# Projection stage of a hybrid decoder step: half 0 as three 256-column matmuls per weight tile, and the sample's convolution taps and pooling sums on GpSimd

## The chip, the cores and the metric

The kernel runs on one core of one Trainium2 chip. The metric is the device time of one execution in microseconds (us), the median of several runs. A profiled execution gives a trace: one record for each instruction on each engine. The engines are PE (TensorE, with PEld for its weight loads), DVE (VectorE), ACT (ScalarE), POOL (GpSimd) and SP (SyncE, which here issues the DMAs). Each engine takes its instructions in the order in which they stand in its own queue.

## The reference

One layer of a decoder step in float32, for 1024 prompt tokens and 8 x 8 sample tokens:

```
x = x + 0.5 * swiglu(rmsnorm(x, norm_ffn1), ffn1_w_in, ffn1_w_out)
hn = rmsnorm(x, norm_mix)
proj = hn @ w_in                       # 1024 -> 8224: u, z, xbc, dt, gate logits
u_ext = [pool_hist, u]                 # trailing-window means of 2, 4, 8, 16 rows, minus u
xp = [conv_hist, xbc]                  # y = b + sum_k xp[:, k:k+T] * w[k];  silu(y)
...                                    # pooling branch, SSD scan, gates, out projection
x = x + mix
x = x + 0.5 * swiglu(rmsnorm(x, norm_ffn2), ffn2_w_in, ffn2_w_out)
y = rmsnorm(x, norm_final)
```

The outputs are y, the last 15 rows of `u_ext`, the last 3 rows of `xp` (the new pooling and convolution states) and the SSD states. The change touches the product `hn @ w_in` and what is done with u and xbc right after it.

## The kernel before

Channels lie on the partitions and tokens along the free dimension. The tokens are worked on as two halves: half 0 holds 512 prompt tokens, half 1 the other 512 and the 64 sample tokens (`NTOK = (512, 576)`).

**Stages.** A first feed-forward block, the projection stage (`in_proj`), the mixing stage (pooling branch, SSD scan, merge, output projection), a second feed-forward block. The projection stage runs in this trace from about 871 us to 1523 us.

**A pair.** `proj_pair` makes two 128-channel rows, `ia` and `ib`, of the projection for both halves by a Winograd-form product: seven products instead of eight, in the order 1, 2, 6, 5, 7, 3, 4 (`PRODUCTS`). There are 29 pairs that hold both halves, and one of half 1 alone: gates (kind g), and in each of four groups three pairs of xbc (kind c), one of u (kind u) and two of z (kind z). So 12 pairs feed the convolution and 4 the pooling.

**A product.** `wino` (line 467) does product p for half 0 and then for half 1, over four 128-row weight tiles k. Float32 accuracy comes from splitting weight and data into a high and a low part, `wh`, `wl` and `xh`, `xl`, and adding wh*xh, wh*xl and wl*xh. Half 1 has 288 columns in a product and does these as three 288-column matmuls, into one range of a PSUM bank. Half 0 has 256 columns. Its high and low parts lie side by side, so that wh*[xh|xl] is one matmul of 512 columns and wl*xh one of 256, and the bank holds two sums of 256 columns that have still to be added. Every matmul loads its own weights. The banks A, B, C of each half are the six buffers of the tag `pd`; A collects products 1, 6, 7 and 4, B product 2, C products 5 and 3.

**Taking the sums out of PSUM.** After each product, `after` calls `leave` (line 1097). For half 1 this is one ACT copy (products 1, 6, 5, 4) or one DVE add (2, 7, 3) of 288 columns into the rows' tiles `ra`, `rb`. For half 0 the copies and adds have 512 columns and go to two scratch tiles `t` and `v` (lines 1120, 1122, 1125, 1127, 1129, 1132), and after products 2, 7 and 3 a POOL add of the two 256-column pieces writes `ra` or `rb` (lines 1123, 1130, 1133). Product 4 of half 0 is an ACT copy and a DVE add of 256 columns (lines 1135, 1136).

**Weights.** `wino_weights` (line 426) makes seven weight tiles of the four raw ones (`wraw`, 6 buffers): four sums `s` on POOL (line 437, 4 buffers), and for each tile a rounded copy `wh` on ACT (line 443) and the rest `wl` on DVE (line 444), 3 buffers each.

**After a row is done** (`done`, after products 3 and 4), work is queued with `post` and fed by a worker between products. `post_conv` does the convolution: ACT makes `b + w0*x` (line 936), DVE adds three taps (line 940), ACT applies silu (line 942) and a DMA writes the result. In half 1 the 64 sample tokens are separate small instructions: POOL copies them with their history into a tile `crs` (lines 931, 932), ACT and DVE do 64-column taps. `post_u` does the window sums by doubling on DVE (line 955; line 959 for the sample, whose rows lie in `urs`), the mean minus u (lines 966, 972) and a split into high and low parts. `state_out` makes the new states: a PE transpose `pst` (line 167) of the last columns of the row's tile, an ACT copy `so` (line 1039), DMAs. In `done` it is queued ahead of `post_conv` or `post_u`.

**Order of the queues.** The program is recorded with a model of time (`tick`, `post`), and a scheduler sets each engine's queue; instructions in `tc.high_priority` blocks (the weights' and `leave`) are drawn ahead. What stands in a queue is fixed before the run.

Of the kernel before, what the change touches and what calls it, by code (L numbers as in the profile page):

```python
# [14 lines left out]
P = 128  # L15
# [46 lines left out]
def tile_hybrid_pool_ssd_macaron(  # L62
# [401 lines left out]
            out.append(raw)  # L464
        return out

    def wino(weights, nk, xs, after):


        banks = [[None] * 3 for _ in xs]  # L470
        for (p, b), (wh, wl) in zip(PRODUCTS, weights):
            for i, (h, X) in enumerate(xs):
                n = NPAIR[h]
                new = banks[i][b] is None
                if new:
                    banks[i][b] = psum("pd", "pw" + p)
                out = banks[i][b][:, :n]
                if h == 0:
                    both = banks[i][b].rearrange("p (a b) -> p a b", a=2)
                    for k in range(nk):  # L480
                        x = X[p][k]
                        mm(both, wh[:, k, :], x, start=new and k == 0, stop=False, free=True)
                        mm(out, wl[:, k, :], x[:, 0, :], start=False, stop=k == nk - 1, free=True)
                    after(p, i, banks[i])
                    tick()
                    continue
                for k in range(nk):
                    xh, xl = X[p][k]
                    for j, (W, x) in enumerate(((wh, xh), (wh, xl), (wl, xh))):
                        mm(out, W[:, k, :], x, start=new and k == 0 and j == 0, stop=k == nk - 1 and j == 2, free=True)  # L490
                after(p, i, banks[i])
                tick()
# [417 lines left out]
    def post(gen):  # L910
        work.append((pe[0] + RIPE, gen))
# [12 lines left out]
    def post_conv(h, ct, raw, new):  # L924
# [11 lines left out]
            S.activation(o, f(0), AF.Identity, bias=cols[:, i_cb + ct : i_cb + ct + 1], scale=w[0])  # L936
        yield POST
        for j in range(1, 4):
            for o, f in parts:
                V.scalar_tensor_tensor(o, f(j), w[j], o, op0=ALU.mult, op1=ALU.add)  # L940
            yield POST
        S.activation(t[:, :N], t[:, :N], AF.Silu)
        dma(convd[h][ct], t[:, :N])
# [2 lines left out]
    def post_u(h, k, raw, smp):  # L946
# [6 lines left out]
        while sh < w:  # L953
# [2 lines left out]
                            cur[:, sh - 1 : HIST + 512 - sh], op=ALU.add)  # L956
            if h == 1:
                nxs = smp[1 + q]
                V.tensor_tensor(nxs[:, :, 2 * sh - 1 :], curs[:, :, 2 * sh - 1 :],
                                curs[:, :, sh - 1 : HIST + NT - sh], op=ALU.add)  # L960
                curs, q = nxs, 1 - q
            yield POST
# [33 lines left out]
    def done(kind, i, h, raw):  # L996
# [25 lines left out]
    outs = {}  # L1022

# [31 lines left out]
    def proj_pair(kind, ia, ib, xs):  # L1055
# [22 lines left out]
        def after(p, i, bk):  # L1078
# [17 lines left out]

        def leave(p, h, n, o, af, as_, bf, bs, *bk):

            f, s_ = slice(0, n), slice(n, 2 * n)
            A, B, C = bk  # L1100
            if h == 1:
                A, B, C = (x[:, :n] if x is not None else None for x in bk)
                if p == "1":
                    S.copy(af, A)
                elif p == "2":
                    V.tensor_tensor(af, B, af, op=ALU.add)
                elif p == "6":
                    S.copy(as_, A)
                elif p == "5":
                    S.copy(bs, C)  # L1110
                elif p == "7":
                    V.tensor_tensor(bs, A, bs, op=ALU.add)
                elif p == "3":
                    V.tensor_tensor(as_, C, as_, op=ALU.add)
                else:
                    S.copy(bf, A)
            else:
                t, v = o["t"][:, : 2 * n], o["v"][:, : 2 * n]
                if p == "1":
                    S.copy(t, A)  # L1120
                elif p == "2":
                    V.tensor_tensor(t, B, t, op=ALU.add)
                    G.tensor_tensor(af, t[:, f], t[:, s_], op=ALU.add)
                elif p == "6":
                    S.copy(v, A)
                elif p == "5":
                    S.copy(t, C)
                elif p == "7":
                    V.tensor_tensor(t, A, t, op=ALU.add)  # L1129
                    G.tensor_tensor(bs, t[:, f], t[:, s_], op=ALU.add)  # L1130
                elif p == "3":
                    V.tensor_tensor(v, C, v, op=ALU.add)
                    G.tensor_tensor(as_, v[:, f], v[:, s_], op=ALU.add)
                else:
                    S.copy(t[:, s_], A[:, s_])
                    V.tensor_tensor(bf, A[:, f], t[:, s_], op=ALU.add)

        wino(wino_weights(W, 0, 4, 4, c0 + ia * P, c0 + ib * P), 4, xs, after)

    def in_proj(prep):  # L1140

# [636 lines left out]
```

## Time and profile before

| | |
|---|---|
| median of 3 runs | 2937.12 us (2936.72 to 2939.24) |
| profiled execution | 2939.05 us, of which the trace's span is 2937.3 us |
| PE busy | 2828.8 us, 96% of the span, 18494 matmuls and as many weight loads |
| DVE busy | 1784.7 us, 61% |
| ACT busy | 1385.2 us, 47% |
| POOL busy | 993.0 us, 34% |
| mean share of 16 DMA engines | 54% |

How to read it: matmuls are pipelined, so each record is longer than the distance to the next one's start; the distance between starts is what a matmul costs in a stream. Shares over the span mix stages with different limits, so the views are asked for the projection stage alone. In the view of groups a line shows the line of the kernel, the engine, the operation, output<-inputs, the shape, the count, then the busy time in us with the mean of one in ns, and the idle time of the engine just before, with what ended it. In the view of waits a line shows who waited for whom: us in total, times, longest us. A timeline's row shows start, duration, engine, line, operation, and the count of merged instructions.

### The profile page before, as it was taken

Reading aid. Unit: us, or ns where it says so; the run is one execution under the profiler, and the core shown is the slowest. Engines: PE = TensorE matmul, PEld = TensorE weight load, DVE = VectorE, ACT = ScalarE, POOL = GpSimd, SP = SyncE. Lnnn points to the kernel's source line nnn. Section 1 sums busy time; section 2 is a strip of 40 time slices with the busy share of each in tenths; the row PEclk is TensorE's granted clock in tenths of the full one; section 3 lists DMA queues with packets and bytes.
Section 4 is the critical chain, followed back from the end, with each engine's and each line's share of the span. In section 5 each row is a group of like instructions: output and inputs, shape, how many; then the busy total and the mean of one; then the engine's idle time right before and its main releaser. Section 6 shows DMA issues by size and latency. Waiting matters only on the chain.

```text
span 2937.3 us, 51029 instructions
## 1 busy us (share of the span) xinstructions
PE 2828.8 (96%) x18494; PEld 2570.2 (88%) x18494; DVE 1784.7 (61%) x2843; ACT 1385.2 (47%) x3024; POOL 993.0 (34%) x1011
## 2 busy tenths in 40 slices
PE   7999999999999999999989999898999999999998
PEld 6999999789989989898977887677999999987898
DVE  6655555434484687887976877766665544453422
ACT  5444444323354555564556766566233444442422
POOL 6434444000133455454422332323234444440000
PEclk9999999999999999999999999999999999999999
DMA  4575554856445555543367777786774532236652
GB/s 134 166 224 182 160 172 132 277 188 194 112 126 163 159 179 159 183 127 124 98 221 240 235 235 232 229 271 184 237 241 153 161 98 77 81 101 212 218 156 72
DMA packets 530332, 507.97 MB, mean 173 GB/s; under 512 B 36884, under 2 KB 374664, under 8 KB 530072
## 3 DMA queue, kind: packets, MB, share of 16 engines
q1 hardware_dynamic: 530064, 504.72, 54.0%
q8 instruction: 145, 2.38, 0.3%
q14 instruction: 107, 0.88, 0.1%
q10 hardware_dynamic: 16, 0.00, 0.0%
HBM read 361.77 MB, written 143.05 MB: 172 GB/s over the span
## 4 chain that ended last, share of the span: by engine, by line
PE 44%; DVE 6%; ACT 3%; DMA 3%; issue 1%; POOL 1%; SPq 1%; POOLq 0%; ACTq 0%; DVEq 0%
PE pw L163 19%; PE po L163 9%; PE pso L163 4%; PE pwo L163 3%; PE pbp L163 3%; PE pg L163 1%; PE pu L163 1%; ACT ab L1357 1%; PE pyd L163 1%; DVE wl L444 1%; DVE ct L940 1%; PE pst L163 1%; DMA wraw<-in_ffn_w_in_dram 0%; DVE xs L1504 0%; DVE ab L1359 0%
## 5 line engine op out<-in xcount | busy, mean ns | idle before, releaser
L163 PE MATMUL pw<-X,wh 128*128 128x288 f32 (+1 forms) x2484 | 624.0, 330 | 11.9 <-ACT t L1120 5.3
L163 PE MATMUL pw<-X,wl 128*128 128x288 f32 (+1 forms) x1644 | 472.9, 288 | 0.8 <-DVE wl L444 0.8
L163 PEld LDWEIGHTS pw<-X,wh 128*128 128x128 f32 x2484 | 417.7, 188 | 51.5 <-ACT t L1120 6.7
L163 PE MATMUL pw<-hl,wh 128*128 128x512 f32 x1072 | 390.5, 398 | 3.1 <-DVE t L1129 2.1
L444 DVE TENSOR_TENSOR wl<-s,wh 128x512 fp32r<-128x512 f32 x288 | 223.3, 776 | 200.6 <-ACT wh L443 179.1
L163 PE MATMUL pw<-hi,wh 128*128 128x288 f32 x1120 | 332.1, 297 | 1.3 <-ACT t L596 1.3
L163 PE MATMUL pw<-lo,wh 128*128 128x288 f32 x1120 | 329.7, 294 | 0.0
L163 PE MATMUL pw<-hi,wl 128*128 128x288 f32 x1120 | 329.6, 294 | 0.0
L295 DVE TENSOR_TENSOR wl<-wraw,wh 128x512 fp32r<-128x512 f32 x228 | 164.2, 721 | 249.2 <-ACT wh L294 236.9
L163 PEld LDWEIGHTS pw<-X,wl 128*128 128x128 f32 x1644 | 310.6, 189 | 1.9 <-DVE wl L444 1.8
L437 POOL TENSOR_TENSOR s<-wraw,wraw 128x512 f32<-128x512 f32 x144 | 196.0, 1361 | 333.7 <-DVE wl L444 216.7
L163 PE MATMUL pw<-hl,wl 128*128 128x256 f32 x1072 | 299.6, 280 | 0.2 <-DVE wl L444 0.2
L294 ACT ACTIVATE wh<-wraw 128x512 fp32r<-128x512 f32 x228 | 137.8, 606 | 326.0 <-PE po L163 229.1
L444 DVE TENSOR_TENSOR wl<-wraw,wh 128x512 fp32r<-128x512 f32 x216 | 177.0, 819 | 123.0 <-ACT wh L443 116.3
L443 ACT ACTIVATE wh<-s 128x512 fp32r<-128x512 f32 x288 | 180.8, 629 | 146.4 <-PE pw L163 139.1
L163 PEld LDWEIGHTS pw<-hl,wh 128*128 128x128 f32 x1072 | 201.9, 188 | 40.6 <-DVE t L1129 2.9
L163 PEld LDWEIGHTS pw<-hi,wh 128*128 128x128 f32 x1120 | 210.1, 188 | 12.6 <-ACT t L596 1.8
L163 PE MATMUL po<-hh,wh 128*128 128x288 f32 (+1 forms) x800 | 211.0, 324 | 3.6 <-ACT hh L355 3.4
L163 PE MATMUL po<-hh,wl 128*128 128x288 f32 (+1 forms) x800 | 210.9, 322 | 0.5 <-DMA wl<-part 0.5
L163 PE MATMUL po<-hr,wh 128*128 128x288 f32 (+1 forms) x800 | 210.9, 323 | 0.0
L163 PEld LDWEIGHTS pw<-lo,wh 128*128 128x128 f32 x1120 | 210.2, 188 | 0.0
L163 PEld LDWEIGHTS pw<-hi,wl 128*128 128x128 f32 x1120 | 210.1, 188 | 0.0
(384 smaller groups left out, 6340.7 us busy)
## 6 DMA issues: line engine op xcount, KB each, us to landing
wraw<-in_ffn_w_in_dram SPq DMA_DIRECT2D x188, 256.0 KB
wh<-part SPq DMA_DIRECT2D x156, 256.0 KB
wl<-part SPq DMA_DIRECT2D x156, 256.0 KB
wraw<-in_w_in_dram SPq DMA_DIRECT2D x144, 256.0 KB
wraw<-in_ffn_w_out_dram SPq DMA_DIRECT2D x120, 256.0 KB
part<-ph SPq DMA_DIRECT2D x80, 256.0 KB
part<-pr SPq DMA_DIRECT2D x80, 256.0 KB
ab<-acsd SPq DMA_DIRECT2D x64, 256.0 KB
```

What stands on the lines that cost most here:

```text
L163: T.matmul(out, lhsT, rhs, start=start, stop=stop, skip_group_check=free)
L294: S.activation(wh, raw, AF.Copy)
L295: V.tensor_tensor(wl, raw, wh.bitcast(F32), op=ALU.subtract)
L437: G.tensor_tensor(t, a, b, op=op)
L443: S.activation(wh, a, AF.Copy)
L444: V.tensor_tensor(wl, a, wh.bitcast(F32), op=ALU.subtract)
L940: V.scalar_tensor_tensor(o, f(j), w[j], o, op0=ALU.mult, op1=ALU.add)
L1357: S.activation(ab[:L, i, :], ab[:L, i, :], AF.Relu, bias=acs[:L, hc + q * hq + i : hc + q * hq + i + 1], scale=-1.0)
```

## The change

Three things change, all in the projection stage.

1. **Half 0's products.** `proj_pair` passes `beside=False` to `wino`. Half 0 then takes the path of half 1: wh*xh, wh*xl and wl*xh are three matmuls of 256 columns into one 256-column range. `leave` loses its branch for half 0: copies and adds of 256 columns go straight into `ra` and `rb`. The tiles `t` and `v`, the 512-column copies and adds and the three POOL adds of each pair are gone. The feed-forward blocks call `wino` as before.
2. **The sample's small work on POOL.** In `post_conv` each 64-column tap of the sample becomes a POOL product into a new small tile `cm` (2 buffers) and a POOL add. In `post_u` the sample's window sums go from DVE to POOL.
3. **`state_out` behind the post.** In `done`, `state_out` is queued after `post_conv` or `post_u`, no longer ahead of it.

```diff
-    def wino(weights, nk, xs, after):
+    def wino(weights, nk, xs, after, beside=True):
...
-                if h == 0:
+                if h == 0 and beside:
                     both = banks[i][b].rearrange("p (a b) -> p a b", a=2)
                     for k in range(nk):
                         x = X[p][k]
                         mm(both, wh[:, k, :], x, start=new and k == 0, stop=False, free=True)
                         mm(out, wl[:, k, :], x[:, 0, :], start=False, stop=k == nk - 1, free=True)
...
                 for k in range(nk):
-                    xh, xl = X[p][k]
+                    xh, xl = X[p][k] if h else (X[p][k][:, 0, :], X[p][k][:, 1, :])
                     for j, (W, x) in enumerate(((wh, xh), (wh, xl), (wl, xh))):
                         mm(out, W[:, k, :], x, start=new and k == 0 and j == 0, stop=k == nk - 1 and j == 2, free=True)
...
         for j in range(1, 4):
-            for o, f in parts:
-                V.scalar_tensor_tensor(o, f(j), w[j], o, op0=ALU.mult, op1=ALU.add)
+            V.scalar_tensor_tensor(t[:, :512], raw[:, j : j + 512], w[j], t[:, :512], op0=ALU.mult, op1=ALU.add)
+            for o, f in parts[1:]:
+                m = small((P, NB, NT), "cm", 2)
+                G.tensor_tensor(m, f(j), w[j].unsqueeze(2).broadcast_to([P, NB, NT]), op=ALU.mult)
+                G.tensor_tensor(o, o, m, op=ALU.add)
             yield POST
...
-                V.tensor_tensor(nxs[:, :, 2 * sh - 1 :], curs[:, :, 2 * sh - 1 :],
+                G.tensor_tensor(nxs[:, :, 2 * sh - 1 :], curs[:, :, 2 * sh - 1 :],
                                 curs[:, :, sh - 1 : HIST + NT - sh], op=ALU.add)
...
             if h == 1:
                 smp = new
+            post(post_conv(h, i, raw, smp))
+            if h == 1:
                 state_out(kind, i, raw[:, 512:579])
-            post(post_conv(h, i, raw, smp))
...
+            post(post_u(h, i, raw, smp))
+            if h == 1:
                 state_out(kind, i, raw[:, 512:591])
-            post(post_u(h, i, raw, smp))
...
-                if h == 0:
-                    out[i].update(t=fx(name="t"), v=fx(name="v"))
...
         def leave(p, h, n, o, af, as_, bf, bs, *bk):
 
-            f, s_ = slice(0, n), slice(n, 2 * n)
-            A, B, C = bk
-            if h == 1:
-                A, B, C = (x[:, :n] if x is not None else None for x in bk)
...
+            A, B, C = (x[:, :n] if x is not None else None for x in bk)
+            if p == "1":
+                S.copy(af, A)
+            elif p == "2":
+                V.tensor_tensor(af, B, af, op=ALU.add)
+            elif p == "6":
+                S.copy(as_, A)
+            elif p == "5":
+                S.copy(bs, C)
+            elif p == "7":
+                V.tensor_tensor(bs, A, bs, op=ALU.add)
+            elif p == "3":
+                V.tensor_tensor(as_, C, as_, op=ALU.add)
             else:
-                t, v = o["t"][:, : 2 * n], o["v"][:, : 2 * n]
-                if p == "1":
-                    S.copy(t, A)
-                elif p == "2":
-                    V.tensor_tensor(t, B, t, op=ALU.add)
-                    G.tensor_tensor(af, t[:, f], t[:, s_], op=ALU.add)
...
+                S.copy(bf, A)
 
-        wino(wino_weights(W, 0, 4, 4, c0 + ia * P, c0 + ib * P), 4, xs, after)
+        wino(wino_weights(W, 0, 4, 4, c0 + ia * P, c0 + ib * P), 4, xs, after, beside=False)
```

The queues show it at three places. On PE, the first state transpose of the stage (`pst`, of row `ra` of the first xbc pair, half 1; `pw` is a product's bank, its number tells the bank). Before, it stands behind half 1's last matmuls of that pair's product 4 (`pw_2031`) and ahead of product 1 of the next pair (`pw_2070`):

```order
L163 MATMUL pw_2031_10998<-hi_9091,wh_11177 128x288
L163 MATMUL pw_2031_10998<-lo_9092,wh_11177 128x288
L163 MATMUL pw_2031_10998<-hi_9091,wl_11178 128x288
L167 MATMUL pst_2063_11215<-ident,ra_11011 67x128
L163 MATMUL pw_2070_11230<-hl_7838,wh_11226 128x512
L163 MATMUL pw_2070_11230<-hl_7838,wl_11227 128x256
L163 MATMUL pw_2070_11230<-hl_7868,wh_11226 128x512
```

Now it stands inside the next pair, behind product 6 of half 0 (`pw_2058` is that pair's bank A of half 0, `pw_2062` that of half 1):

```order
L163 MATMUL pw_2058_11364<-X_8951,wh_11453 128x256 x2
L163 MATMUL pw_2058_11364<-X_8951,wl_11454 128x256
L163 MATMUL pw_2058_11364<-X_8999,wh_11453 128x256 x2
L163 MATMUL pw_2058_11364<-X_8999,wl_11454 128x256
L167 MATMUL pst_2081_11471<-ident,ra_11123 67x128
L163 MATMUL pw_2062_11384<-X_9310,wh_11453 128x288 x2
L163 MATMUL pw_2062_11384<-X_9310,wl_11454 128x288
```

Between the two places lie five half-products (1 and 2 of both halves, 6 of half 0), and each pair of a 512- and a 256-column matmul has become three of 256 columns.

On POOL, one xbc pair's weight sums `s` and what stands between them, before (`ra`, `rb` with `t`, `v` are half 0's adds; `crs` are the copies of the sample):

```order
L437 TENSOR_TENSOR s_2195_11904<-wraw_11823,wraw_11825 128x512
L1123 TENSOR_TENSOR ra_11544<-t_11546 128x256
L437 TENSOR_TENSOR s_2196_11906<-s_2195_11904,wraw_11819 128x512
L931 COPY crs_11846<-hs_9780 128x8x3
L437 TENSOR_TENSOR s_2213_11983<-wraw_11819,wraw_11823 128x512
L437 TENSOR_TENSOR s_2217_12017<-wraw_11821,s_2196_11906 128x512
L1004 MEMSET rb_11545 128x3
L1130 TENSOR_TENSOR rb_11545<-t_11546 128x256
L1005 COPY chist<-rb_11545 128x3
L1007 COPY rb_11569<-chist 128x3
L1133 TENSOR_TENSOR ra_11544<-v_11547 128x256
```

and now, around the four sums of a pair (`cm`, `ct` are the sample's taps):

```order
L942 TENSOR_TENSOR cm_11632<-crs_11589,cols 128x64
L437 TENSOR_TENSOR s_2135_11788<-wraw_11695,wraw_11697 128x512
L437 TENSOR_TENSOR s_2136_11790<-s_2135_11788,wraw_11691 128x512
L437 TENSOR_TENSOR s_2147_11864<-wraw_11691,wraw_11695 128x512
L1007 MEMSET rb_11378 128x3
L437 TENSOR_TENSOR s_2150_11899<-wraw_11693,s_2136_11790 128x512
L943 TENSOR_TENSOR ct_11588<-ct_11588,cm_11609 128x64
L1008 COPY chist<-rb_11378 128x3
L943 TENSOR_TENSOR ct_11588<-ct_11588,cm_11632 128x64
L1010 COPY rb_11398<-chist 128x3
L942 TENSOR_TENSOR cm_11652<-crs_11589,cols 128x64
L943 TENSOR_TENSOR ct_11588<-ct_11588,cm_11652 128x64
```

The 256-column adds are gone from between the sums; six small taps of each sample row have come in, and those of the second row stand behind all four sums of the next pair.

On ACT, the silu of that second row (`ct_11588`) and what follows it now:

```order
L936 ACTIVATE ct_11588<-crs_11589,cols 128x64
L443 ACTIVATE wh_11699<-wraw_11691 128x512
L936 ACTIVATE ct_11678<-ra_11377,cols 128x512
L945 ACTIVATE ct_11588<-ct_11588 128x576
L443 ACTIVATE wh_11743<-wraw_11693 128x512
L936 ACTIVATE ct_11685<-ra_11397,cols 128x512
L1116 COPY rb_11378<-pw_2058_11364 128x256
```

The silu (line 945) waits for the last POOL tap of the fence above, where before it waited for DVE, and the copy that empties half 0's bank A after product 4 (line 1116) stands behind it.

More of the change, by code (lines that the diff above doesn't have):

```diff
@@ L1097, in leave @@
         def leave(p, h, n, o, af, as_, bf, bs, *bk):
-            f, s_ = slice(0, n), slice(n, 2 * n)
-            A, B, C = bk
-            if h == 1:
-                A, B, C = (x[:, :n] if x is not None else None for x in bk)
-                if p == "1":
-                    S.copy(af, A)
-                elif p == "2":
[L1106 to L1116, printed above, removed]
-            else:
-                t, v = o["t"][:, : 2 * n], o["v"][:, : 2 * n]
[L1119 to L1136, printed above, removed]
```

## The prediction

> **What bounds the kernel now.** On the page PE is busy for 96% of the span, so a change pays only by what PE streams or by what it waits for. I asked first for the busy time in stretches of the projection stage:
>
> ```profile
> core 0: us, PE busy (x) PEld busy (x) DVE busy (x) ACT busy (x) POOL busy (x), PEclk, DMA share, GB/s
> 1160.00:1330.00 170.00, 165.18 (x1095) 153.43 (x1094) 148.11 (x225) 95.48 (x196) 87.10 (x109) 1.00 0.47 150
> sum 663.00, PE 646.30 PEld 600.97 DVE 512.71 ACT 356.22 POOL 304.25; mean PE 129.26 PEld 120.19 DVE 102.54 ACT 71.24 POOL 60.85
> ```
>
> In 663 us around the stage PE is idle for 663.0 - 646.3 = 16.7 us. DVE is the next busiest, 77% over all and 148.11/170 = 87% in the second stretch; POOL has 46%. Then the waits of PE in the stage (who waited for whom: us, times, longest):
>
> ```profile
> PE pst L167 <- DVE ra L1114: 6.7, 8, 1.4
> PE pw L163 <- ACT t L1120: 5.3, 5, 3.0
> PE pw L163 <- DVE t L1129: 2.1, 2, 1.3
> PE pw L163 <- DVE wl L444: 1.0, 3, 0.5
> PE pw L163 <- ACT v L1125: 0.4, 1, 0.4
> ```
>
> Together 15.5 us in 19 stops. Eight are the state transpose, which waits for the last DVE add of its row; the others wait for half 0's tiles to leave PSUM or for a low weight part. The timeline shows what the longest stop costs beside its idle time:
>
> ```profile
> 1470.01 0.29 PE L163 MATMUL pw<-hi,wl 128*128 128x288 f32 x1
> 1473.28 0.79 PE L163 MATMUL pw<-X,wh 128*128 128x512 f32 x1 [2.98 <-ACT t L1120]
> ...
> 1474.08 0.63 PE L163 MATMUL pw<-X,wh 128*128 128x512 f32 x1
> ...
> 1474.72 0.63 PE L163 MATMUL pw<-X,wh 128*128 128x512 f32 x1
> ```
>
> A pair of a 512- and a 256-column matmul takes 0.64 us here, against 0.35 us in the stream below: four such pairs at a low rate, 4 x 0.29 = 1.2 us. And each stop loses the overlap of two records, some 0.16 us (a 288-column record is 0.29 us long and the next usually starts after 0.13). What kept ACT was DVE:
>
> ```profile
> 1471.96 0.63 ACT L355 ACTIVATE dh<-dd 128x512 fp32r<-128x512 f32 x1 [4.06 <-DVE dd L970]
> 1472.50 0.24 ACT L1039 COPY so<-pst 79x128 f32<-79x128 f32 x1
> 1472.64 0.58 ACT L1120 COPY t<-pw 128x512 f32<-128x512 f32 x1
> ```
>
> ACT stood 4.06 us for a DVE chain of the pooling, and the copy that PE needed stood behind it. So the stage is PE's stream plus some 20 us of stops (15.5 + 19 x 0.16 + 1.2 = 19.7), and DVE's queue is what is late at most of them.
>
> **The change, part by part.** *PE's stream.* 29 pairs x 7 products x 4 tiles = 812 times a 512- and a 256-column matmul become three of 256. The columns are the same, 768, but there is a third matmul with a third weight load. The trace has no run of 256-column matmuls; its nearest rows are these starts:
>
> ```profile
> 1483.75 0.39 PE L163 MATMUL pw<-hl,wh 128*128 128x512 f32 x1
> 1483.98 0.28 PE L163 MATMUL pw<-hl,wl 128*128 128x256 f32 x1
> ...
> 1485.16 0.29 PE L163 MATMUL pw<-hi,wh 128*128 128x288 f32 x1
> ...
> 1486.76 0.39 PE L163 MATMUL pw<-hl,wh 128*128 128x512 f32 x1
> ```
>
> Four pairs of half 0 take 1485.16 - 1483.75 = 1.41 us, 0.3525 each or 0.459 ns a column; twelve matmuls of half 1 take 1.60 us, 0.1333 each or 0.463 ns a column. Three times 256 at 0.463 is 0.3556 us, 3.1 ns more; 812 times that is +2.5 us, which I take, since 288 columns is the nearest row that repeats one width. The low bound is 0 (0.459 a column). The high bound is three full 288-column distances, 0.400 us, if it is the weight load that sets 0.133 and not the columns: +0.0475 x 812 = +39 us. Against that end speaks
>
> ```profile
> 1644.00 1.05 PE L163 MATMUL pyo<-bc,hst 128*128 128x128 f32 x8
> L163 PE MATMUL pyo<-bc,hst x224: 270/275/421, 1571.1 to 2029.8; 128*128 128x128 f32 x112
> L163 PE MATMUL pw<-hl,wl 128*128 128x256 f32 x1072 | 299.6, 280 | 0.2 <-DVE wl L444 0.2
> ```
>
> Eight matmuls, each with a weight load of the same size, within 1.05 us, with the last record 0.275 long: (1.05 - 0.275)/7 = 0.111 us each, less than the 0.119 that I give one of 256 columns. The Trainium skill's page "TensorE: Matmul & The Clock Gate" (Back-to-back issue gap) speaks against the change too: a warm matmul costs its columns plus a fixed 2.5 ns. By it the third matmul would cost 812 x 2.5 ns = +2.0 us where columns alone say 0; the row of 288 agrees with a small fixed cost.
>
> *State transposes.* They now stand five half-products later, 2 x 1.6 + 3 x 1.41 = 7.4 us by the starts above. Their longest wait was 1.4 us, so all eight should go: 6.7 + 8 x 0.16 = -8.0 us (at worst half, if DVE is late elsewhere: -4.0).
>
> *Work on DVE, ACT and POOL.* The groups in the stage:
>
> ```profile
> L1122 DVE TENSOR_TENSOR t<-pw,t 128x512 f32<-128x512 f32 x29 | 19.8, 682 | 0.9 <-PE pw L163 0.7 <-DMA gd<-rb 0.2
> L1136 DVE TENSOR_TENSOR rb<-pw,t 128x256 f32<-128x256 f32 x29 | 12.1, 418 | 2.3 <-ACT t L1135 1.3
> L940 DVE SCALAR_TENSOR_TENSOR ct<-crs,cols,ct 128x64 f32<-128x64 f32 x72 | 32.2, 447 | 0.0
> L940 DVE SCALAR_TENSOR_TENSOR ct<-crs,cols,ct x72: 267/274/1323, 1006.4 to 1464.7; 128x64 f32<-128x64 f32 x72
> L959 DVE TENSOR_TENSOR urs<-urs x20: 210/326/1385, 1070.8 to 1485.4; 128x176 f32<-128x176 f32 x8, 128x160 f32<-128x160 f32 x6, 128x128 f32<-128x128 f32 x4, 128x64 f32<-128x64 f32 x2
> L1120 ACT COPY t<-pw 128x512 f32<-128x512 f32 x29 | 16.7, 576 | 0.7 <-PE pw L163 0.7
> L1135 ACT COPY t<-pw 128x256 f32<-128x256 f32 x29 | 10.3, 356 | 3.0 <-PE pw L163 2.7
> L1123 POOL TENSOR_TENSOR ra<-t 128x256 f32<-128x256 f32 x29 | 30.4, 1049 | 31.6 <-DVE t L1122 25.0 <-issue 6.6
> L1130 POOL TENSOR_TENSOR rb<-t 128x256 f32<-128x256 f32 x29 | 27.9, 962 | 49.3 <-DVE t L1129 49.3
> L1133 POOL TENSOR_TENSOR ra<-v 128x256 f32<-128x256 f32 x29 | 25.8, 889 | 27.4 <-DVE v L1132 27.3
> L932 POOL COPY crs<-ra 128x64 f32<-128x64 f32 x12 | 3.4, 280 | 1.2
> L437 POOL TENSOR_TENSOR s<-wraw,wraw 128x512 f32<-128x512 f32 x58 | 82.1, 1416 | 142.5 <-DVE wl L444 87.1 <-DMA wraw<-in_w_in_dram 22.2 <-DVE ct L940 13.7
> ```
>
> DVE: three 512-column adds at 0.682 become 256-column ones at the 0.418 of line 1136, whose own add goes: 29 x (3 x 0.264 + 0.418) = 35 us. With the 72 taps (32.2) and the 20 sums (at the median 0.326: 6.5) it loses 74 of its 513 us and falls to 66%. ACT loses 29 x 3 x (0.576 - 0.356) = 19 us. POOL loses 30.4 + 27.9 + 25.8 = 84 us and gains 144 taps and 20 sums. A tap has 64 columns: a copy of that size takes 0.28, and a straight line through the two-input operations of 512 and 256 columns (1.416 and 0.967, the mean of the three) gives 0.63; I take 0.5, so 72 us, and 0.8 for a sum, which the same line gives for 170 columns: 16 us. POOL stays where it was, at 84 gone and 88 come (bounds 56 and 107).
>
> *The other 11 stops* cost 15.5 - 6.7 = 8.8 us, 11 x 0.16 = 1.8 and the slow 1.2, so 11.8 us. They come where DVE, or ACT behind it, is behind; a DVE freed of a seventh of its work, and half-0 copies that wait for no POOL add, should take half of them, -5.9 (bounds 0 and -11.8). ACT's waits on POOL's adds go with these:
>
> ```profile
> ACT ct L936 <- POOL ra L1133: 27.2, 10, 3.8
> POOL s L437 <- DVE wl L444: 94.1, 36, 7.2
> ```
>
> Sum: 2.5 - 8.0 - 5.9 = -11.4, from the profiled 2939.05 to 2927.6. The runs' median is 1.9 lower than that execution, so I forecast **2926 us**. By the bounds without the 39: from 0 - 8.0 - 11.8 = -20 to 2.5 - 4.0 - 0 = -1.5, so 2917 to 2936 on the median. What follows the stage (DMA landings of the mixing stage's first loads) keeps its order, and I give it nothing.
>
> **The rivals.**
>
> *A wait on POOL takes the place of the old ones (slower).* The sample's second row has its taps behind the next pair's four weight sums. These wait for their buffers, last row above: 2.6 us on average, 7.2 at most. The silu on ACT then waits for POOL, and behind it stands the copy that empties bank A of half 0. That bank is needed by the next pair's product 1, half a product (1.6 us) after product 4 ends; from there PE stands. Twelve xbc pairs, each held 3.6 us (2.6 and two taps), lose 12 x 2.0 = 24 us, against which the 8.0 are still won and nothing else: 2937 + 2.5 + 24 - 8 = 2955. For it: the queue order, and that POOL is slow for its size. Against: the sums' buffers come free with products 6 to 3, ahead of product 4. The Trainium skill's "GPSIMD Engine Reference" (Engine selection) is on its side: elementwise work belongs on VectorE, two-input operations are about twice as slow on GpSimd. The trace agrees (0.97 us here against 0.418 for 256 columns).
>
> *The stops only move.* If DVE's lateness is contention with POOL and DMA waits rather than its own load, PE meets the same stops elsewhere: 2937 + 2.5 - 4 = 2936. For it: POOL stays as busy, and the small tap on DVE takes 447 ns on average where its median is 274 and its longest 1323, so DVE is held up now and then by something outside it.
>
> *All stops go*: 2937 - 19.7 = 2917.
>
> *The weight load sets the pace*: +39 - 14 = 2962.
>
> **How the numbers follow.** Forecast 0.44, stops move 0.20, POOL wait 0.22, all gone 0.10, weight load 0.04. A difference under 0.2%, 5.9 us, is about what a measurement of this kernel can't tell from none, so faster means below 2931.2. The forecast's own range (2917 to 2936) is to nine tenths below that: 0.40; with "all gone" 0.50, and 0.03 of the moved stops. Slower, above 2943: the POOL wait, the load, and 0.01 of the moved: 0.27. The rest, 0.20, is the same. Range: 2914 to 2952; it reaches to the POOL case with two thirds of its price.
>
> **What would show it.** In the changed profile: no wait of `pst` for the DVE add of product 3; half-0 matmuls starting 0.117 to 0.119 us apart; DVE near 440 us in the same stretch, POOL near 305; PE's waits in the stage about 6 us. Wrong if the 256-column starts are 0.13 apart (load), if ACT's silu waits on POOL for over 1.6 us again and again with PE waiting for line 1116's copy, or if PE still waits for half 0's copies as long as before.

## The result, and the profile after

| | median of the runs, us | ratio to before, 95% interval |
|---|---|---|
| before (4 runs beside the change) | 2938.18 (2936.72 to 2939.93) | |
| after (4 runs) | 2922.75 (2920.70 to 2923.54) | 0.9945 (0.9932 to 0.9957) |

The change makes the kernel 15.4 us faster. The forecast was 2926, its own range 2917 to 2936. The profiled execution of the changed kernel took 2922.54 us, its span 2920.7. The busy time in the 663 us that the prediction looked at:

```profile
core 0: us, PE busy (x) PEld busy (x) DVE busy (x) ACT busy (x) POOL busy (x), PEclk, DMA share, GB/s
860.00:1523.00 663.00, 654.51 (x5143) 648.93 (x5141) 443.77 (x701) 355.36 (x742) 312.77 (x435) 1.00 0.50 161
```

DVE came down from 513 to 444 us (forecast near 440), POOL went from 304 to 313 (forecast near 305), and the same stretch now holds 17 us of the next stage. ACT, forecast to lose 19 us, stands at 355 after 356; some 10 of the 355 lie in those 17 us. PE's waits from 870 to 1520 us (who waited for whom: us, times, longest):

```profile
PE pxT L167 <- DMA xs<-cv: 3.9, 4, 3.0
PE pgm L163 <- ACT rb L1116: 0.9, 1, 0.9
PE pw L163 <- DVE wl L444: 0.7, 1, 0.7
```

The first two rows belong to the mixing stage's first work. Of before's 15.5 us in 19 stops one stop of 0.7 us is left. Neither the state transposes (`pst`) nor the half-0 copies appear. The first matmul of the mixing stage (`pgm`) starts at 1505.7 us in place of 1523.0.

The stream itself became longer. Eight 256-column matmuls of half 0, on the timeline:

```profile
1049.29 0.28 PE L163 MATMUL pw<-X,wh 128*128 128x256 f32 x1
1049.41 0.28 PE L163 MATMUL pw<-X,wl 128*128 128x256 f32 x1
1049.53 0.40 PE L163 MATMUL pw<-X,wh 128*128 128x256 f32 x2
1049.77 0.28 PE L163 MATMUL pw<-X,wl 128*128 128x256 f32 x1
1049.89 0.40 PE L163 MATMUL pw<-X,wh 128*128 128x256 f32 x2
1050.13 0.28 PE L163 MATMUL pw<-X,wl 128*128 128x256 f32 x1
1050.25 0.27 PE L167 MATMUL pst<-ident,ra 128*67 128x128 f32 x1
```

They take 1050.25 - 1049.29 = 0.96 us, 0.120 each, so three take 0.360 us where the old pair took 0.3525.

The groups of POOL and DVE that answer to those of before:

```profile
L942 POOL TENSOR_TENSOR cm<-crs,cols 128x64 f32<-128x64 f32 x72 | 46.6, 659 | 0.8
L943 POOL TENSOR_TENSOR ct<-ct,cm 128x64 f32<-128x64 f32 x72 | 40.7, 566 | 23.3 <-ACT ct L936 20.5 <-POOL ra L1007 0.7
L1112 DVE TENSOR_TENSOR rb<-pw,rb 128x256 f32<-128x256 f32 x29 | 12.1, 419 | 1.7 <-PE pw L163 1.6
```

A tap's operation on POOL takes 0.57 to 0.66 us on average for 64 columns (0.5 was put in), the shortest 0.29; why they differ so much is seen with DVE's taps below. The feared wait of ACT's silu (line 945) for POOL is there:

```profile
ACT ct L945 <- POOL ct L943: 27.1, 14, 3.2
POOL s L437 <- DVE wl L444: 147.8, 50, 11.9
```

and 11 of its 14 times are longer than the 1.6 us that the prediction named as a sign of being wrong. The other half of that sign, PE waiting for line 1116's copy, is missing in the stage: no stop of PE there follows from it.

To compare kernels I added up, over every PE start from 870 to 1500 us, the distance to the next start beyond 0.233, 0.117 or 0.133 us (after a projection matmul of 512, 256 or 288 columns). What exceeds by over 0.06 us is a stop with its slow matmuls, the rest is the stream. Before: stream -0.5, stops 27.8 us. After: stream +4.8, stops 6.1. The floor of this count is about 5.6, which it gives for a kernel below with no stop of the stage in its list of waits. So some 22 us of stops went, about the 19.7 that the prediction had counted, and 5 to 6 us of stream came. (The floor is 59 distances too long by some 0.1 us each, nearly all of them beside a transpose in the stream.)

### The profile page after: what moved, and what is told of

It is laid out like the page before. It is cut to its first block, busy times and chain, and to the rows that moved or that the text cites. A ratio compares the mean times of both kernels' runs of the same rounds, so it can differ in the third digit from the quotient of the medians.

```text
span 2920.7 us, 52612 instructions
## 1 busy us (share of the span) xinstructions
PE 2829.0 (97%) x19306; PEld 2612.3 (89%) x19306; DVE 1715.2 (59%) x2722; ACT 1374.7 (47%) x3024; POOL 1001.9 (34%) x1088
## 4 chain that ended last, share of the span: by engine, by line
PE 47%; DVE 4%; DMA 3%; ACT 2%; issue 1%; SPq 1%; POOL 0%; POOLq 0%; ACTq 0%; DVEq 0%
PE pw L163 24%; PE po L163 9%; PE pso L163 4%; PE pbp L163 3%; PE pwo L163 2%; PE pg L163 1%; PE pu L163 1%; ACT ab L1337 1%; PE pyd L163 1%; PE pst L163 1%; DVE ab L1339 1%; DMA ab<-acsd 0%; PE pyo L163 0%; DVE xs L1484 0%; DMA wh<-part 0%
## 5 line engine op out<-in xcount | busy, mean ns | idle before, releaser
L163 PE MATMUL pw<-X,wh 128*128 128x288 f32 (+2 forms) x2832 | 626.9, 310 | 4.7 <-ACT v L560 3.6
L163 PEld LDWEIGHTS pw<-X,wh 128*128 128x128 f32 x2832 | 461.7, 189 | 27.3 <-ACT v L560 4.5
L163 PE MATMUL pw<-hl,wh 128*128 128x256 f32 (+1 forms) x1536 | 392.1, 328 | 0.9 <-DVE t L564 0.9
L295 DVE TENSOR_TENSOR wl<-wraw,wh 128x512 fp32r<-128x512 f32 x228 | 163.7, 719 | 253.2 <-ACT wh L294 240.3
L163 PEld LDWEIGHTS pw<-hl,wh 128*128 128x128 f32 x1536 | 259.0, 189 | 21.8 <-DVE t L564 1.1
L444 DVE TENSOR_TENSOR wl<-wraw,wh 128x512 fp32r<-128x512 f32 x216 | 168.9, 782 | 137.6 <-ACT wh L443 131.0
```

The lines of the kernel that those rows point to most:

```text
L163: T.matmul(out, lhsT, rhs, start=start, stop=stop, skip_group_check=free)
L295: V.tensor_tensor(wl, raw, wh.bitcast(F32), op=ALU.subtract)
L444: V.tensor_tensor(wl, a, wh.bitcast(F32), op=ALU.subtract)
```

## The experiments

Every kernel was timed in turn with the kernel before; ratios are to it. The kernel before took between 2938 and 2941 us beside them, so small differences between two kernels that were not timed together are better read from the ratios. "Wide" is half 0 as before, a 512- and a 256-column matmul; "narrow" is three of 256. The three parts are numbered as in the section on the change.

### The parts alone

Four kernels: part 3 alone, part 1 alone, part 2 alone, and parts 2 and 3 without 1. The edits are the hunks of the diff:

```diff
# state transposes later, half 0 wide
-                state_out(kind, i, raw[:, 512:579])
             post(post_conv(h, i, raw, smp))
+            if h == 1:
+                state_out(kind, i, raw[:, 512:579])
...
```

> The kernel before with the third part of the change alone: state_out queued behind the post. Theory (the eight waits of pst are stops of their own, 8 us with their restarts, and the later place ends them): 2930 us, no wait of pst on DVE in the stage, the other 11 stops about as before (8.8 us idle). Rival (DVE is late and PE meets it at the next place): 2936 to 2938, the pst waits gone but the waits of pw on ACT and DVE risen by about as much.

```diff
# half 0 narrow
-                if h == 0:
+                if h == 0 and beside:
...
-        wino(wino_weights(W, 0, 4, 4, c0 + ia * P, c0 + ib * P), 4, xs, after)
+        wino(wino_weights(W, 0, 4, 4, c0 + ia * P, c0 + ib * P), 4, xs, after, beside=False)
...
```

> The kernel before with the first part alone: half 0 by three 256-column matmuls, sums of PSUM straight into the rows' tiles; sample's small work on DVE, state_out ahead of the post. Theory (the third matmul costs 812 times some 8 ns, 6.5 us; DVE is freed of 35 us, ACT of its waits for POOL's adds, so most of the 11 other stops go and the pst waits shrink to half): 2938 + 6.5 - 9 - 4 = 2931. Rival (the stops go only when the sample's work leaves DVE too): 2938 + 6.5 - 2 = 2942.

```diff
# sample's taps and sums on POOL, half 0 wide
...
+                G.tensor_tensor(m, f(j), w[j].unsqueeze(2).broadcast_to([P, NB, NT]), op=ALU.mult)
+                G.tensor_tensor(o, o, m, op=ALU.add)
...
-                V.tensor_tensor(nxs[:, :, 2 * sh - 1 :], curs[:, :, 2 * sh - 1 :],
+                G.tensor_tensor(nxs[:, :, 2 * sh - 1 :], curs[:, :, 2 * sh - 1 :],
```

> The kernel before with the second part alone: the sample's taps and window sums on POOL, half 0 wide with its POOL adds. Theory (DVE's load is what makes the stops: 39 us less of it takes about half of the 11 other stops and half of the pst waits): 2938 - 6 - 4 = 2928. Rival (POOL, now at 304 + 100 of 663 us with half 0's adds still in its queue, makes ACT and DVE wait): 2945 or more, waits of ACT on POOL above the 54 us of before.

Parts 2 and 3 together, half 0 wide:

> The change without its first part: sample's work on POOL and state_out later, half 0 wide as before. Theory (no third matmul, so 6.5 us less than the change, if the stops go as there): 2916 to 2920. Rival (half 0's POOL adds and the sample's taps together make POOL late, and stops of pw on ACT and DVE stay at 6 us or more): 2926 to 2930, not below the change's 2922.8.

With two of the last experiments all eight combinations are there. Median us, ratio with its interval:

| | half 0 wide | half 0 narrow |
|---|---|---|
| neither | 2939.54 (before, 9 runs) | 2922.91, 0.9946 (0.9933 to 0.9960) |
| transposes later | 2956.0, 1.0057 (1.0045 to 1.0070) | 2917.96, 0.9928 (0.9915 to 0.9940) |
| sample on POOL | 2963.72, 1.0086 (1.0071 to 1.0101) | 2922.73, 0.9943 (0.9930 to 0.9955) |
| both | 2957.15, 1.0067 (1.0054 to 1.0079) | 2922.75, 0.9945 (0.9932 to 0.9957) (the change) |

The gain is that of the narrow half 0, which alone reaches the changed kernel's time. The two other parts cost 16 to 24 us while half 0 is wide, and between nothing and a gain of 5 us once it is narrow. Of these four expectations only one held, the rival for part 2 alone (2945 or more). Part 1 alone gained more than either of its two allowed (2931, 2942), and the two kernels with the late place in the wide form came out slower than either of theirs.

*Why the later place is slower in the wide kernel.* Its waits on PE:

```profile
PE puh L167 <- ACT so L1041: 10.5, 4, 2.9
PE pw L163 <- DVE wl L444: 6.6, 11, 1.3
PE pw L163 <- ACT t L1122: 6.1, 4, 4.1
```

The wait of `pst` is gone, as the prediction said, and 10.5 us for `puh` have come; with two smaller ones PE's waits in the stage add up to 27.0 us, where before had 15.5. The transposes that make the sample's u history now stand right behind the state transpose and use the same two PSUM buffers (tag `ps`): the second `puh` needs the buffer that ACT's copy `so` has to empty. The timelines of ACT, POOL, DVE and PE around one such stop:

```profile
1051.54 0.68 ACT L942 ACTIVATE ct<-ct 128x576 f32<-128x576 f32 x1 [2.50 <-DVE ct L940]
1052.12 0.57 ACT L1127 COPY v<-pw 128x512 f32<-128x512 f32 x1
1052.59 0.26 ACT L1041 COPY so<-pst 67x128 f32<-67x128 f32 x1
```

```profile
1048.23 1.73 POOL L437 TENSOR_TENSOR s<-wraw,wraw 128x512 f32<-128x512 f32 x1 [4.73 <-DVE wl L444]
```

```profile
1048.73 1.32 DVE L940 SCALAR_TENSOR_TENSOR ct<-crs,cols,ct 128x64 f32<-128x64 f32 x1
1049.97 0.68 DVE L1124 TENSOR_TENSOR t<-pw,t 128x512 f32<-128x512 f32 x1
1050.57 0.73 DVE L940 SCALAR_TENSOR_TENSOR ct<-ra,cols,ct 128x512 f32<-128x512 f32 x1
1051.23 0.27 DVE L940 SCALAR_TENSOR_TENSOR ct<-crs,cols,ct 128x64 f32<-128x64 f32 x1
```

```profile
1052.91 0.46 PE L167 MATMUL puh<-ident,spin 120*128 120x120 f32 x1 [2.16 <-ACT so L1041]
```

Read from the top of the chain: a tap of 64 columns, 0.27 us two rows further down, lasts 1.32 us and ends at 1050.05, right after POOL's weight sum ends (1048.23 + 1.73 = 1049.96). Then DVE does a half-0 add of 512 columns and two more taps. Until then ACT stands in front of the silu (2.50 us), behind which stand a 512-column copy and `so`, and PE stands for `so`. The tap's hold is 1.05 us of this stop of 2.16. Behind such stops PE also streams slowly for a while: the granted clock is 0.50 from 1052.7 to 1056.1 us, one of four such stretches of 3.4 us in this trace's stage; before has one. In the narrow kernels the same transposes stand at the same place, and the list of waits has no `puh`: ACT is on time. That the two shared buffers are the cause is read from the traces; a kernel with buffers of their own for these transposes was not tried.

The long tap is no single case. Of before's 72 small taps, the 38 that ran while POOL had no two-input operation took 0.273 us on average, 0.280 at most. Of the other 34, 23 took longer, up to 1.32 us, and every one of the 23 ended 0.08 us after the end of such a POOL operation: a weight sum or a half-0 add. The Trainium skill's page "SBUF — State Buffer" (Who interferes with whom) has the rule for it: a DVE instruction with two SBUF inputs contends with a GpSimd instruction that reads SBUF, the lock on what they share is exclusive, and a DVE instruction with at most one SBUF input, outside certain modes, is spared. The trace agrees: of the changed kernel's 87 half-0 adds, which read PSUM and one SBUF tile, 37 met a two-input POOL operation and took 0.416 us on average, the other 50 took 0.419.

It goes both ways. In the changed kernel the 127 POOL tap operations that met a DVE operation with two SBUF inputs took 0.65 us on average, the other 17 took 0.31.

*Where the narrow half 0 gains on DVE.* The 72 small taps, the same instructions on the same engine, with half 0 narrow and nothing else changed:

```profile
L940 DVE SCALAR_TENSOR_TENSOR ct<-crs,cols,ct 128x64 f32<-128x64 f32 x72 | 22.2, 308 | 0.0
```

308 ns on average where before had 447. And the busy time of that kernel in the same stretch (columns as above):

```profile
860.00:1523.00 663.00, 655.40 (x5139) 649.10 (x5137) 462.40 (x790) 347.68 (x733) 227.67 (x269) 1.00 0.50 158
```

With half 0 wide DVE has 513 us, with it narrow 462: 51 us less. The 35 that the prediction counted for shorter adds are part of it; the taps' 32.2 - 22.2 = 10 us are time in which DVE no longer stands for POOL (3 long taps are left of the 23).

*Why POOL is too much for the wide kernel.* Waits of the kernel with part 2 alone:

```profile
ACT ct L936 <- POOL ra L1136: 42.2, 11, 5.0
PE pw L163 <- DVE wl L444: 12.6, 21, 1.6
PE pst L167 <- DVE ra L1117: 11.4, 9, 3.8
```

The half-0 add on POOL that completes a row (line 1136) now stands behind the sample's taps: in the seven longest of these waits, 4.2 to 5.0 us, POOL does it without a pause behind the taps of another row. ACT waits for it 42.2 us (27.2 before), and what stands behind ACT and DVE comes to PE's stops. So a wait on POOL does take the place of the old ones, but not the one that the rival of that name described: the silu's wait for the taps is 14.7 us in 5 here, less than the 27.1 in the changed kernel, where it costs nothing. That the times, 2957 and 2964, lie near that rival's 2955 is luck.

### What it is in the wide half 0 that costs

Part 1 takes four things away: POOL's add between PSUM and the finished row, some of DVE's time, two scratch buffers per pair, and the 512-column form of the stream. Each was put back alone on the narrow kernel (part 1 alone, 2922.91), in four kernels that the expectations call h1 to h4, in this order.

```diff
# a POOL step on the way of the row, after products 2, 7 and 3 of half 0
+                    G.tensor_tensor(af, af, ones[:, :1].broadcast_to([P, 256]), op=ALU.mult)
...
```

> e2 (half 0 narrow alone) with a POOL product by one, 256 columns, in place behind the DVE adds of products 2, 7 and 3 of half 0: POOL's 84 us and the hop through POOL's queue are back, no DVE load and no buffer with them. If it was POOL's adds in the rows' path that made the stops (ACT waited 54 us for line 1133 before): 2938 or more, waits of ACT on POOL and stops of pw and pst back to 12 us or more. If it was DVE's load or the buffers t and v: 2923 to 2926.

Measured: 2931.03 us, ratio 0.9967 (0.9954 to 0.9979), between its two expectations: 8 us of the gain are gone by the medians, 6 by the ratios. The transposes wait again:

```profile
PE pst L167 <- DVE ra L1113: 6.2, 7, 1.5
```

Two of these stops, up to 1045.14 us (0.70) and up to 1287.70 us (0.51):

```profile
1042.92 1.05 POOL L1115 TENSOR_TENSOR ra<-ra,ones 128x256 f32<-128x256 f32 x1 [1.44 <-DVE ra L1113]
1043.42 0.64 DVE L940 SCALAR_TENSOR_TENSOR ct<-crs,cols,ct 128x64 f32<-128x64 f32 x1
1043.98 0.74 DVE L940 SCALAR_TENSOR_TENSOR ct<-rb,cols,ct 128x512 f32<-128x512 f32 x1
1044.64 0.44 DVE L1113 TENSOR_TENSOR ra<-pw,ra 128x288 f32<-128x288 f32 x1
...
1285.68 0.82 ACT L936 ACTIVATE ct<-ra,cols 128x512 f32<-128x512 f32 x1 [2.82 <-POOL ra L1115]
1286.53 0.75 DVE L940 SCALAR_TENSOR_TENSOR ct<-ra,cols,ct 128x512 f32<-128x512 f32 x1 [0.80 <-ACT ct L936]
1287.20 0.45 DVE L1113 TENSOR_TENSOR ra<-pw,ra 128x288 f32<-128x288 f32 x1
```

The row that PE waits for is half 1's, whose sums never pass through POOL; its add (line 1113, 288 columns) is late because of what stands ahead of it on DVE. In the second stop that is a tap that waited 0.80 us for ACT, which had waited 2.82 us for POOL's step. In the first DVE has no such pause, but its small tap was held by the step, 0.64 us in place of 0.27. So the step acts in two ways: it stands on the row's way to ACT, and it holds DVE. Of the seven stops three are of the second kind and four of the first, where a hold of 0.36 us is part of the stops' 0.7 to 1.5 and the rest lies in DVE's queue. How the 6 to 8 us divide between the two was not tried; a POOL operation of the same size on a tile that nobody waits for would tell.

```diff
# DVE's time, an in-place pass of 256 columns after products 2, 7, 3 and 4 of half 0
+                    V.tensor_tensor(af, af, af, op=ALU.max)
...
```

> e2 with four DVE operations of 256 columns more per pair, in place (the maximum of a row with itself) behind products 2, 7, 3 and 4 of half 0: DVE's 35 us or somewhat more are back, POOL's are not. If DVE's load made the stops: 2935 to 2942, DVE at 500 us in 663. If it was POOL's hop or the buffers: 2923 to 2927.

Measured: 2931.00 us, 0.9964 (0.9952 to 0.9976), also between its expectations: 8 us by the medians, 5 by the ratios. DVE has 502 us in the stretch, near before's 513; the stops stand at the copies out of PSUM and at the transposes:

```profile
PE pw L163 <- ACT ra L1099: 2.0, 2, 1.1
PE pst L167 <- DVE ra L1113: 2.0, 2, 1.1
PE pw L163 <- ACT ra L1105: 1.7, 2, 1.0
```

```diff
# the two scratch buffers, held as long as before
+                    out[i].update(t=fx(name="t"), v=fx(name="v"))
...
```

> e2 with the two scratch buffers of half 0 taken again for the length of each pair, written and read by four POOL operations of one or two columns: 15 of 17 buffers are left as before, loads are not back. If the buffers made the stops: 2935 or more, with DVE and ACT waiting at the first writes of rows and scratch tiles. If not: 2923 to 2926.

Measured: 2923.75 us, 0.9943 (0.9931 to 0.9956). The buffers cost nothing that shows.

```diff
# the old stream, the new way out of PSUM: the second 256 columns of the bank are not added in
-        wino(wino_weights(W, 0, 4, 4, c0 + ia * P, c0 + ib * P), 4, xs, after, beside=False)
+        wino(wino_weights(W, 0, 4, 4, c0 + ia * P, c0 + ib * P), 4, xs, after)
```

> e2 with half 0's products as one 512- and one 256-column matmul again, but only the first 256 columns of the bank taken out: it leaves wh*xl out of half 0's projection. It prices the third matmul alone. By the starts in the changed kernel's trace (0.120 us from one 256-column matmul to the next, against 0.3525 for the pair): 812 x 7.5 ns = 6.1 us less, 2916.8. If the columns alone counted: 2922.9.

Measured: 2922.97 us, 0.9938 (0.9924 to 0.9952), the same by the median and some 2 us less by the ratio, where 6.1 less were expected. By the count of starts the stream is 6.2 us shorter (-1.2 in place of +5.0), and the stops are 5.2 us longer (14.9 in place of 9.7), mostly for the transposes:

```profile
PE pst L167 <- DVE ra L1109: 5.3, 6, 1.7
```

So the third matmul's 6 us were not the price that its length says. Given back, most of them turn into stops; presumably because DVE and ACT have less time per product, which the runs don't separate.

### Both burdens at once, the other parts, and a better version

The last four kernels put the POOL step and DVE's passes together, put parts 2 and 3 each on the narrow half 0, and take away the stop that leads the list of waits right behind the stage.

> Half 0 narrow, with both burdens put back at once: a GpSimd pass over 256 columns behind products 2, 7 and 3 of half 0 (as in h1, +8 us alone) and four in-place DVE passes of 256 columns per pair (as in h2, +8 us alone). Theory A, the two burdens simply add: 2923 + 8 + 8 = 2939, PE waits for the state transpose and for the half-0 tiles about 8 to 10 us together, like before's 15.5 less what the scratch tiles t and v did. Theory B, they make each other worse, since a late DVE add makes GpSimd late and the other way round: above 2943, with stops of over 20 us, as the wide form has before's stops and saves 6 us of stream on top. Theory C, they hide behind each other (whichever is later decides): 2931, stops as in h1.

Measured: 2945.46 us, 1.0019 (1.0010 to 1.0028). Together they cost 22.5 us, alone 8.1 each, by the medians. In ratios the excess over the sum is 0.0073 - 0.0021 - 0.0018 = 0.0034, give or take 0.0024 (the four half-widths added in squares): theory B, if not by much. The waits look like before's:

```profile
PE pst L167 <- DVE ra L1117: 7.0, 8, 1.5
PE pw L163 <- ACT ra L1099: 3.8, 4, 1.8
PE pw L163 <- ACT ra L1107: 2.6, 3, 1.4
PE pw L163 <- DVE wl L444: 2.1, 2, 1.1
```

By the count of starts it has before's stops (26.8 and 27.8 us) and the narrow stream (+5.0 and -0.5); the profiled execution, 2948.85 us, is one of its slowest. So the POOL step and DVE's time between them are enough to bring back what the wide half 0 costs. They are no exact copy of it: DVE's passes read two SBUF inputs, where the wide adds read PSUM and one, so POOL can hold them too.

> The change without its GpSimd part: half 0 narrow, state transposes later, the sample's taps and sums still on DVE. If the narrow half 0 alone makes the gain and the late place costs nothing once the rows are in time: 2921 to 2925, no wait of the state transpose for the DVE add of product 3. If the late place costs what it cost in the wide form (its transposes then use the two buffers that the u transposes need, 16 us): about 2930 to 2938 with waits of the u transposes for the copy of the state.

Measured: 2917.96 us, 0.9928 (0.9915 to 0.9940), 3 us below the better of its expectations. No wait of the projection stage is left in PE's list; `pgm` starts at 1505.2 us, against 1509.2 with part 1 alone. The late place of the transposes is worth these 4 us in the stage, once the rows are in time.

> The change without the late place of the state transposes: half 0 narrow, the sample's taps and sums on GpSimd. Theory one (GpSimd was only dangerous on top of the half-0 adds): 2921 to 2925, and the transposes wait for the add of product 3 about 1 to 3 us in all. Rival (GpSimd's work on the sample makes DVE and ACT late whatever half 0 does, as it did in the wide form, +24 us): above 2930.

Measured: 2922.73 us, 0.9943 (0.9930 to 0.9955). The transposes wait 2.6 us in 2 stops; the work on POOL neither helps nor hurts the total. The rival, over 2930, is out. Against this kernel the late place of the change gains 2.8 us in the stage (`pgm` at 1508.5 and 1505.7) and nothing in the total.

The changed kernel as a whole is 4.8 us above the one without part 2. In the projection stage they differ by 0.5 us (`pgm` at 1505.7 and 1505.2). The rest arises in the mixing stage, whose code is the same in both: from the first `pgm` to the last state product 498.6 us and 494.8. The kernels of this study but the next spread from 493 to 499 there. The spread goes roughly with the granted clock: added up, the stretches at half clock take 27 us of the mixing stage in the kernel with the old stream put back (494.5 us), 31 in that with the POOL step (492.7), 38 without part 2 (494.8), 41 in the change (498.6) and 48 with part 2 alone (498.7). What brings these stretches about was not tried.

```diff
         ahead_d = []
-        for k in range(6):
+        for k in range(8):
             ahead_d.append(load_d(0, k))
```

> The change, with the operands of all eight pooling blocks loaded ahead of the mixing stage instead of six. In the changed kernel the first matmul of the mixing stage that waits for such a load stands 4.4 us. If the load is what is late: that wait goes, 2917 to 2919. If the wait only moves to the next stage's other loads, or the additional tiles are short in their pool: 2921 to 2925, or slower.

Measured: 2913.40 us (2912.99 to 2917.93), 0.9917 (0.9903 to 0.9930), the fastest here and below what was expected (2917 to 2919). The stop in question, in the waits of the changed kernel:

```profile
PE pgm L163 <- DMA d<-dh: 4.4, 1, 4.4
```

and on its timeline, with the slow matmuls behind it, two in 1.37 us where a pair had 0.61:

```profile
1513.25 0.61 PE L163 MATMUL pgm<-d,wh 128*128 128x512 f32 x2
...
1524.50 1.37 PE L163 MATMUL pgm<-d,wh 128*128 128x512 f32 x2 [4.37 <-DMA d<-dh]
```

With all eight loads ahead this wait is gone, and PE has 36.0 us of work from 1490 to 1530 us in place of 30.8. The gain of 9 us is twice the wait, and the clock shows where more of it comes from. The stretch behind the stop, in the changed kernel and in this one (columns as above; PEclk 0.71 and 1.00):

```profile
1518.00:1535.00 17.00, 11.93 (x41) 8.51 (x42) 6.99 (x11) 10.38 (x22) 1.04 (x1) 0.71 0.85 271
1518.00:1535.00 17.00, 15.45 (x80) 11.61 (x79) 9.13 (x15) 12.34 (x28) 3.12 (x3) 1.00 0.81 252
```

In the changed kernel the clock is halved for 10.2 us from 1517.6 us on, around stops of 3.0 and 4.4 us; with the loads ahead there is one stop of 1.5 us, and the clock stays. Over the whole mixing stage 20.5 us are at half clock in place of 41.0, and the stage takes 489.5 us in place of 498.6. Before has the same wait (4.3 us), so this gain doesn't belong to the change; on the kernel before, and on the version without part 2, it wasn't tried.

## Why the prediction was right, point by point

*What bounds the stage.* Right: PE's stream plus some 20 us of stops that come from DVE's and ACT's lateness. The stops went and the time with them. That 2926 lies within 4 us of the result is in part luck, as the next points show: the stream was put 3.6 us too low and the stops that go 5.9 too low, and the two errors partly cancel.

*PE's stream, +2.5 us: too small.* It measured 812 x 7.5 ns = +6.1 us by the starts shown, +5.3 by the count over the stage, within the bounds 0 and 39. The step that failed is the choice of "288 columns as the nearest row" with the time taken in proportion to the columns: 256 of them take 0.120 us, not 0.1185; against 288 columns that is 0.0133 us less where proportion asks for 0.0148, so a matmul here has a part that doesn't shrink with its columns. The weight load did not bind (0.133 would have shown it). The Trainium skill's page "TensorE: Matmul & The Clock Gate" (Back-to-back issue gap) gives its fixed 2.5 ns as part of the gap of an isolated matmul, not of a stream with weight loads. By it the term would have been +2.0 us, as far off: a third matmul costs 7.5 ns here. Nor did the row of 288 agree with it, as the prediction says: an estimate by that page's formula gives 288 columns 0.1225 us, and the row has 0.1333.

*State transposes, -8.0 us: the amount came, the reason given did not hold.* The step "They now stand five half-products later ... so all eight should go" took the place of the transposes as the cause. The later place alone makes the kernel 16.5 us slower, by a queue that the prediction did not look at: the `puh` transposes and their two PSUM buffers behind ACT's `so`. What removed most of these waits is that the rows are finished in time (6.7 us in 8 stops before, 1.5 in 3 with part 1 alone). The late place then adds 3 to 4 us in the stage, about the low bound of that term.

*The other eleven stops, -5.9 us as half of 11.8: too small.* All but one of 0.7 us went. The two causes that the step named both have a price, 5 to 8 us each when put back: "a DVE freed of a seventh of its work", and "half-0 copies that wait for no POOL add", though POOL's add also held DVE, which this step left out. The sum with the measured stream and all stops gone is 6.1 - 8.0 - 11.8 = -13.7, and the runs gave -15.4, the sum of the prediction -11.4.

*POOL at 84 gone and 88 come.* The balance was about right (304 before, 313 after), but it is not the balance that matters. The 84 us lay on the way from PSUM to the finished row, the taps lie beside it; both hold DVE. The relief of DVE by part 2, on which 39 of the 74 us rested, brought nothing measurable. Either DVE had time enough with part 1 alone, or POOL's new work took back what the relief gave; the runs don't tell which.

*The rivals.* POOL's wait is real (27.1 us on ACT) and without price here, as ACT's copies are not late for any PSUM bank. With the wide half 0 another wait on POOL, for the row's own add, decides. "The stops only move" is what part 3 alone does, and worse: they grow. Its remark that something outside DVE holds the small taps is right, and it is POOL. "All stops go" is what parts 1 and 3 do; that their 2918 meets its 2917 is luck, since that rival left out the 5 us of stream. The range's upper end is not what its reason says: two thirds of the POOL case's 24 us end at 2947.5, and 2952 takes in 20.5 of them.

## What to carry to other kernels

When several engines hand a row on, try taking the slowest hand-over out of the row's way, even if PE gets more to do: six us more of stream bought some 22 us of stops. Look also at what else the engine that is relieved was holding up: here POOL's adds held DVE's taps. A later place in a queue frees a wait only if what now stands beside it, here two PSUM buffers shared with other transposes, is on time too. And try the parts of a change apart in both settings: two of these three were slower alone, and one of them adds nothing at the end.

## What the hardware showed beyond that

- A 256-column matmul with its own weight load starts the next one after 0.120 us, one of 288 columns after 0.133. Splitting 512 + 256 columns into three matmuls costs 7.5 ns per weight tile in this stream.
- A two-input operation of 64 columns takes 0.29 us at the least on POOL and 0.27 on DVE; 256 columns take 0.73 at the least on POOL, 512 take 1.27. The averages in the groups (0.57 to 0.66 for 64 columns, 0.89 to 1.05 for 256) are longer because the two engines hold each other.
- DVE's two-input operations on SBUF data last up to 1.32 us for 0.27 when a two-input POOL operation runs; a small tap that is held ends 0.08 us after it. With the half-0 adds gone from POOL, DVE's small taps went from 447 to 308 ns on average.
- Beside long stops of PE the granted clock was 0.50, in stretches of 3.4 us or a multiple: 10.2 us around the stops of 3.0 and 4.4 us in the changed kernel.
